# Attention scores of 96 heads on one core: blocks of eight heads for blocks of four, loads of 64 partitions for loads of 128, and all copies of a head on ScalarE

## The chip, the cores and the metric

The kernel runs on one core of one Trainium2 chip; the other cores are idle. The metric is the device time of one execution in microseconds (us): the median of ten runs before the change, and the median of the changed kernel's runs after it. One execution of each kernel is also recorded by the hardware profiler; all rows below come from that execution. Its span, from the first recorded instruction to the last, is a little shorter than its time.

## The reference

```python
batch, n_heads, seq, head_dim = 8, 12, 1024, 64
q, k: float32 [8, 12, 1024, 64]
np.einsum('bhid,bhjd->bhij', q, k).astype(np.float32)
```

For each of the 96 pairs of batch and head, 1024 query rows of 64 numbers are multiplied with 1024 key rows. The result of one head is a 1024 x 1024 matrix in float32, 4 MB. All inputs together are 50.33 MB, all outputs 402.65 MB.

## The kernel before

A "head" below is one of the 96 matrices. The kernel goes through them in order, in blocks: `sizes = [1, 1, 2, 2, ...]`, where a block with G has two halves of G heads each, so the first two blocks have 2 heads and the other 23 have 4. GMAX is 2. In a block, the heads of the first half have their transposed q and k on partitions 0 to 63 and those of the second half on 64 to 127.

The stages of a block, each on its own engine:

- **Loads** (`Block.load`, line 74). For each half and each of q and k there is one DMA into a tile `x_sb` of 128 partitions; partition p holds 8G consecutive rows of the input. For G = 2 that is 16 rows of 64 floats, 4 KB per partition, 512 KB per DMA. `in_pool` has 5 such tiles (each with q and k of one half). The first three blocks are loaded into the tile `early`, which borrows one of the output buffers.
- **Casts** (`cast_rows`, line 93, for the first two blocks, and `cast_quads`, line 115, for the others). GpSimd turns the rows into float16 in the tile `half_sb`. `cast_quads` works on 32 partitions at a time and moves each piece so that a later transpose of 32 x 32 squares gives the head's matrix transposed. `half_pool` has 2 tiles, and a block takes one.
- **Transposes** (`transpose_rows`, lines 140 and 143, for the first two blocks; `transpose_quads`, line 132, for the others). The first kind is eight TensorE transposes through PSUM and a VectorE copy. The second is a VectorE instruction, two of them for q and two for k of a block: each reads 1024 contiguous elements per partition of `half_sb` and writes them to `qT` or `kT` with a step of R = 8G elements. `tr_pool` has two tiles of each name.
- **Scores** (`scores`, line 159). For each head there are four steps u; in each, TensorE does four products of 64 x 128 by 64 x 512 into a PSUM tile of 128 x 2048 floats. There are two such tiles.
- **Copies** from PSUM to the output tile `o_sb` (128 partitions x 32 KB). ScalarE does them (line 170), except for every fourth head of a block (n = 3), which VectorE does (line 168). For the very first head the two engines share each step (lines 165 and 166). `out_pool` has four output tiles.
- **Store** (line 174). SP issues one DMA of 4 MB per head, 32 KB per partition.

The order is written out: `pin` keeps every instruction in program order on its engine, and the program itself is one loop over blocks and heads. While block i is multiplied, the transposes of block i+1 are put into its heads by the dictionary `side` (after step 0 of heads 0, 1 and 2; head 2 takes two). After the copies of a head, ScalarE issues one load (two after the first head), taken from the list `stream` of the loads of all later blocks. Six loads of this list are issued ahead of the loop, three by SP and three by ScalarE. The casts of block i+3 are put on GpSimd's queue at the end of block i. An instruction waits for its data and for its buffer to be free; the waiting instruction holds up what is queued behind it on its engine. For ScalarE a load that waits holds up the next head's copies.

Of the kernel before, what the change touches and what calls it, by code (L numbers as in the profile page):

```python
# [9 lines left out]
F16 = mybir.dt.float16  # L10
F32 = mybir.dt.float32
P = 128
# [3 lines left out]
def kernel(  # L16
# [6 lines left out]
    nc = tc.nc  # L23

    B, H, S, D = q.shape
    NT = S // P
    BH = B * H
    GMAX = 2
    assert D == 64 and NT == 8 and BH % (2 * GMAX) == 0


# [5 lines left out]
    kf = k.rearrange("b h s d -> (b h s) d")  # L37
    of = out.rearrange("b h i j -> (b h) i j")

    sizes = [1, 1] + [GMAX] * (BH // (2 * GMAX) - 1)  # L40
    assert 2 * sum(sizes) == BH
    PE_BLOCKS = 2

    consts = ctx.enter_context(tc.tile_pool(name="consts", bufs=1))
    ident = consts.tile([P, P], F16)

    in_pool = ctx.enter_context(tc.tile_pool(name="in_pool", bufs=5))
    half_pool = ctx.enter_context(tc.tile_pool(name="half_pool", bufs=2))
    tr_pool = ctx.enter_context(tc.tile_pool(name="tr_pool", bufs=2))
    out_pool = ctx.enter_context(tc.tile_pool(name="out_pool", bufs=4))  # L50
    po_pool = ctx.enter_context(
        tc.tile_pool(name="po_pool", bufs=2, space=bass.MemoryType.PSUM)
    )
# [2 lines left out]
    pin = tc.keep_in_program_order  # L56

    class Block:
# [4 lines left out]

        def load(self, n, eng):
            half, x = divmod(n, 2)
            if self.raw[half] is None:
                x_sb = in_pool.tile([P, 2, self.elems], F32, tag="x")
                self.raw[half] = x_sb  # L70
            start = (self.first + half * self.G) * S
            src = (qf, kf)[x][start : start + self.G * S]
            pin(
                eng.dma_start(  # L74
                    out=self.raw[half][:, x],
                    in_=src.rearrange("(p r) d -> p (r d)", p=P),
                )
            )

# [19 lines left out]

        def cast_quads(self, half_sb):
            self.half_sb = half_sb
            for half in range(2):
                raw = self.raw[half].rearrange(
                    "p x (r h d) -> p x r h d", h=2, d=32
                )
                for h in range(2):
                    q0 = 32 * (2 * half + h)
                    dst = half_sb[q0 : q0 + 32].rearrange(  # L110
                        "p (x b r d) -> p x b r d", x=2, b=4, d=32
                    )
                    for b in range(4):
                        pin(
                            nc.gpsimd.tensor_copy(  # L115
                                out=dst[:, :, b],
                                in_=raw[32 * b : 32 * b + 32, :, :, h],
                            )
                        )

        def alloc(self):
            self.qT = tr_pool.tile([P, GMAX * S], F16, tag="qT")
            self.kT = tr_pool.tile([P, GMAX * S], F16, tag="kT")

        def transpose_quads(self, part, x):
            src = self.half_sb.rearrange("p (x n) -> p x n", x=2)[:, x]
            src = src.rearrange("p (b r i) -> p b r i", b=4, i=32)
            dst = (self.qT, self.kT)[x].rearrange(
                "c (b i r) -> c b r i", b=4, i=32, r=self.R
            )  # L130
            two = slice(2 * part, 2 * part + 2)
            pin(nc.vector.transpose(out=dst[:, two], in_=src[:, two]))  # L132

        def transpose_rows(self, x):
            assert self.G == 1
# [7 lines left out]
            pin(nc.vector.tensor_copy(out=dst, in_=src))  # L143


        def scores(self, n, by_vector, side):
            half, g = divmod(n, self.G)
            cs = slice(half * D, (half + 1) * D)

            qT = self.qT.rearrange("c (g m t) -> c g t m", t=NT, m=P)  # L150
            kT = self.kT.rearrange("c (g j) -> c g j", j=S)
            o_sb = out_pool.tile([P, NT, S], F32, tag="out")
            for u in range(NT // 2):
                ps = po_pool.tile([P, 2, S], F32, tag="po")
                for tt in range(2):
                    for j in range(2):
                        js = slice(j * 512, (j + 1) * 512)
                        pin(
                            nc.tensor.matmul(  # L159
                                ps[:, tt, js], qT[cs, g, 2 * u + tt], kT[cs, g, js]  # L160
                            )
                        )
                dst = o_sb[:, 2 * u : 2 * u + 2]
                if self.first + n == 0:
                    pin(nc.scalar.copy(out=dst[:, 0], in_=ps[:, 0]))  # L165
                    pin(nc.vector.tensor_copy(out=dst[:, 1], in_=ps[:, 1]))  # L166
                elif by_vector:
                    pin(nc.vector.tensor_copy(out=dst, in_=ps))  # L168
                else:
                    pin(nc.scalar.copy(out=dst, in_=ps))  # L170
                if u in side:
                    side[u]()
            pin(
                nc.sync.dma_start(  # L174
                    out=of[self.first + n].rearrange("(p t) j -> p (t j)", p=P),
                    in_=o_sb.rearrange("p t j -> p (t j)"),
                )
            )

    blocks, first = [], 0  # L180
# [4 lines left out]

    early = out_pool.tile([P, NT, S], F32, tag="out")
    raw = early.rearrange("p t j -> p (t j)")  # L190
    at = 0
    for b in blocks[:3]:
        for half in range(2):
            b.raw[half] = raw[:, at : at + 2 * b.elems].rearrange(
                "p (x n) -> p x n", x=2
            )
            at += 2 * b.elems
        for n in range(4):
            b.load(n, (nc.sync, nc.scalar)[n % 2])
    stream = [(b, n) for b in blocks[3:] for n in range(4)]  # L200

    def next_load(eng):
        if stream:
            b, n = stream.pop(0)
            b.load(n, eng)

    for n in range(6):
        next_load((nc.sync, nc.scalar)[n % 2])
    make_identity(nc, ident)

    def to_half(i):
        if i < len(blocks):
            if i == 1:
                half_sb = blocks[0].half_sb[:, 4 * blocks[0].elems :]
            else:
                half_sb = half_pool.tile([P, 8 * GMAX * NT * D // 2], F16, tag="half")
            if i < PE_BLOCKS:
                blocks[i].half_sb = half_sb
                blocks[i].cast_rows(half_sb)
            else:  # L220
                blocks[i].cast_quads(half_sb)

    for i in range(3):
        to_half(i)

    blocks[0].alloc()
    for x in range(2):
# [1 line left out]
    for i, b in enumerate(blocks):  # L229
        nxt = blocks[i + 1] if i + 1 < len(blocks) else None  # L230
        if nxt:
            nxt.alloc()
        heads = 2 * b.G
        for n in range(heads):
            side = {}
            if nxt and i + 1 < PE_BLOCKS:
                side = {3: lambda: nxt.transpose_rows(n)}
            elif nxt and n < 3:
                parts = [(p, x) for p in range(2) for x in range(2)]
                some = parts[n : n + 1 + (n == 2)] if heads == 4 else parts[2 * n :][:2]  # L240
                side = {0: lambda: [nxt.transpose_quads(*s) for s in some]}
            b.scores(n, n == 3, side)
            if i == n == 0:
                next_load(nc.scalar)
            next_load(nc.scalar)
            if i == 0 and n == heads - 1:
                to_half(3)
        if i > 0:
            to_half(i + 3)


# [28 lines left out]
```

## Time and profile before

| | before |
|---|---|
| median of 10 runs | 1068.32 us (1067.97 to 1069.05) |
| the profiled execution, its own time | 1068.53 us |
| its span | 1066.8 us |
| busy TensorE (matmul) | 705.0 us, 66% |
| busy VectorE | 617.7 us, 58% |
| busy ScalarE | 528.9 us, 50% |
| busy GpSimd | 385.7 us, 36% |
| bytes moved by DMA | 453.29 MB, 425 GB/s over the span |

In the profile PE is TensorE, DVE is VectorE, ACT is ScalarE, POOL is GpSimd and SP is SyncE. A line of digits shows 40 equal slices of the span, each digit the busy share in tenths. A group's row gives the line of the kernel, the engine, the operation, output and input with partitions x elements and type, the count, then busy time and mean duration in ns, and after the second bar the engine's idle time ahead of these instructions and what ended most of it. The chain follows back from the last instruction what each step waited for. Rows of windows give, for a stretch of the span, its length, the busy time and count of TensorE's matmuls and weight loads, VectorE, ScalarE and GpSimd, TensorE's clock as a share, the busy share of the DMA engines and the GB/s that they moved.

### The profile page before, as it was taken

What the parts mean: (1) busy time and instruction counts of PE and PEld (TensorE: products, weight loads), DVE (VectorE), ACT (ScalarE), POOL (GpSimd) and SP (SyncE); (2) the same over time, 40 slices, a digit from 0 to 9 for tenths busy, and PEclk for the clock granted to TensorE, in tenths of its full rate; (3) what the DMA queues carried; (4) which work ended last, traced back from release to release, by engine and by line L of the source; (5) the groups of instructions that cost most, each with busy time, mean ns of one, the idle gap of its engine ahead of it and who ended that gap; (6) DMA issues with size and microseconds to landing.
All of it is one profiled execution on the core that took longest, in us unless ns stands there. A gap on an engine that the chain in (4) does not pass through costs nothing.

```text
span 1066.8 us, 4547 instructions
## 1 busy us (share of the span) xinstructions
PE 705.0 (66%) x1568; PEld 237.7 (22%) x1568; DVE 617.7 (58%) x192; ACT 528.9 (50%) x293; POOL 385.7 (36%) x382
## 2 busy tenths in 40 slices
PE   5997566657666675766657576675766766677750
PEld 2332122222222221222222122221222222222210
DVE  3886729366393673845738458385483754955330
ACT  3867264364543645537355373553735546447530
POOL 7894341633416334253352433524335243300000
DMA  9999999999999999999999999999999999999996
GB/s 377 428 424 436 417 423 437 427 434 430 431 429 432 431 431 431 431 428 429 431 428 432 430 431 429 432 430 426 432 429 430 430 430 431 432 434 433 431 434 276
DMA packets 28248, 453.29 MB, mean 425 GB/s; under 512 B 3136, under 2 KB 3136, under 8 KB 15936
## 3 DMA queue, kind: packets, MB, share of 16 engines
q1 hardware_dynamic: 15120, 406.33, 88.6%
q10 hardware_dynamic: 13104, 46.67, 10.8%
q8 instruction: 12, 0.20, 0.1%
q14 instruction: 12, 0.10, 0.0%
HBM read 50.33 MB, written 402.65 MB: 425 GB/s over the span
## 4 chain that ended last, share of the span: by engine, by line
DMA 76%; ACT 11%; PE 6%; DVE 3%; issue 0%; DVEq 0%; ACTq 0%; SPq 0%
DMA out_dram<-o_sb 69%; ACT o_sb L170 11%; DMA x_sb<-in_q_dram 6%; PE ps L159 5%; DVE o_sb L168 3%; DMA early<-in_k_dram 1%; DVE o_sb L166 0%; DVEq L275 0%; ACT o_sb L165 0%; ACT L165 0%; DVE kT L143 0%; PE ps L140 0%; ACTq L170 0%; SPq L174 0%; ACTq L74 0%
## 5 line engine op out<-in xcount | busy, mean ns | idle before, releaser
L159 PE MATMUL ps<-kT,qT 64*128 64x512 f16 x1536 | 701.1, 617 | 320.8 <-ACT o_sb L170 207.3
L170 ACT COPY o_sb<-ps 128x2048 f32<-128x2048 f32 x288 | 523.7, 1868 | 480.8 <-DMA out_dram<-o_sb 389.1
L115 POOL CAST half_sb<-x_sb 32x1024 f16<-32x1024 f32 x352 | 363.8, 1033 | 524.3 <-DVE kT L132 385.2
L168 DVE COPY o_sb<-ps 128x2048 f32<-128x2048 f32 x92 | 204.3, 2284 | 396.3 <-DMA out_dram<-o_sb 391.1
L159 PEld LDWEIGHTS <-qT 64*128 64x128 f16 x1536 | 234.4, 157 | 785.7 <-issue 783.4
L132 DVE STREAM_TRANSPOSE kT<-half_sb 128x1024 f16<-128x1024 f16 x46 | 218.1, 4742 | 0.0
L132 DVE STREAM_TRANSPOSE qT<-half_sb 128x1024 f16<-128x1024 f16 x46 | 212.3, 4615 | 0.0
L115 POOL CAST half_sb<-early 32x1024 f16<-32x1024 f32 x16 | 16.5, 1033 | 2.3 <-DMA early<-in_k_dram 1.6
L140 PE MATMUL ps<-ident,half_sb 128*128 128x128 f16 x32 | 3.9, 309 | 7.2 <-POOL half_sb L93 6.4
L166 DVE COPY o_sb<-ps 128x1024 f32<-128x1024 f32 x4 | 4.8, 1222 | 6.5 <-ACT o_sb L165 6.5
L165 ACT ACT_TABLE_LOAD x1 | 1.3, 1283 | 11.6 <-DMA early<-in_k_dram 11.6
L143 DVE COPY kT<-ps 128x1024 f16<-128x1024 f16 x2 | 2.4, 1220 | 7.6 <-PE ps L140 7.6
L143 DVE COPY qT<-ps 128x1024 f16<-128x1024 f16 x2 | 2.4, 1220 | 7.4 <-PE ps L140 7.4
L93 POOL CAST half_sb<-early 128x512 f16<-128x512 f32 x8 | 4.7, 613 | 3.7 <-DMA early<-in_q_dram 3.6
L165 ACT COPY o_sb<-ps 128x1024 f32<-128x1024 f32 x4 | 4.0, 1014 | 3.0 <-PE ps L159 3.0
L140 PEld LDWEIGHTS <-half_sb 128*128 128x128 f16 x32 | 3.3, 142 | 8.8 <-POOL half_sb L93 6.4
masks.py:199 POOL TENSOR_SCALAR_AFFINE_SELECT ident<-ident 128x128 f16<-128x128 f16 x1 | 0.3, 292 | 0.1
masks.py:197 POOL MEMSET ident<- 128x128 f16 x1 | 0.2, 204 | 0.3 <-POOLq L264 0.3
L264 POOL MEMSET const-float32-0.0<- 128x1 f32 x1 | 0.1, 97 | 0.2 <-issue 0.2
L264 POOL MEMSET const-bfloat16-1.0<- 128x1 bf16 x1 | 0.1, 100 | 0.0
L264 POOL MEMSET const-uint8-127<- 128x1 uint8 x1 | 0.1, 100 | 0.0
L264 POOL MEMSET const-float32-1.0<- 128x1 f32 x1 | 0.1, 98 | 0.0
## 6 DMA issues: line engine op xcount, KB each, us to landing
out_dram<-o_sb SPq DMA_DIRECT2D x96, 4096.0 KB, 36.1
x_sb<-in_k_dram ACTq DMA_DIRECT2D x44, 512.0 KB, 25.2
x_sb<-in_q_dram ACTq DMA_DIRECT2D x41, 512.0 KB, 25.6
x_sb<-in_q_dram SPq DMA_DIRECT2D x3, 512.0 KB, 10.2
early<-in_k_dram ACTq DMA_DIRECT2D x4, 256.0 KB, 5.2
early<-in_q_dram SPq DMA_DIRECT2D x4, 256.0 KB, 4.8
early<-in_q_dram SPq DMA_DIRECT2D x2, 512.0 KB, 7.2
early<-in_k_dram ACTq DMA_DIRECT2D x2, 512.0 KB, 7.3
```

Source lines behind the costliest of these rows:

```text
L93: nc.gpsimd.tensor_copy(out=self.halves[x][:, :, half], in_=self.raw[half][:, x].rearrange("p (r d) -> p r d", d=D),)
L115: nc.gpsimd.tensor_copy(out=dst[:, :, b], in_=raw[32 * b : 32 * b + 32, :, :, h],)
L132: pin(nc.vector.transpose(out=dst[:, two], in_=src[:, two]))
L140: pin(nc.tensor.transpose(t_ps[:, t], self.halves[x][:, t], ident))
L143: pin(nc.vector.tensor_copy(out=dst, in_=src))
L159: nc.tensor.matmul(ps[:, tt, js], qT[cs, g, 2 * u + tt], kT[cs, g, js])
L165: pin(nc.scalar.copy(out=dst[:, 0], in_=ps[:, 0]))
L166: pin(nc.vector.tensor_copy(out=dst[:, 1], in_=ps[:, 1]))
L168: pin(nc.vector.tensor_copy(out=dst, in_=ps))
L170: pin(nc.scalar.copy(out=dst, in_=ps))
L264: nc = _bacc.Bacc("TRN2", target_bir_lowering=False, num_devices=1)
```

## The change

- GMAX is 4: after blocks of 2, 2 and 4 heads come eleven blocks of 8 heads. A half of such a block has 8 KB per partition and input.
- A load of a half is cut into two pieces, of partitions 0 to 63 and 64 to 127, so that a DMA stays at 512 KB. There is still one load after each head, and two after heads 0, 2, 3, 4 and 5.
- `in_pool` has 3 tiles (each twice as large), `half_pool` has 3 and a block takes two of them, `out_pool` has 3.
- The casts of a half are queued as soon as its loads have been issued, up to two or three blocks ahead. They handle 32 x 2048 elements each.
- A transpose of an eight-head block handles 128 x 2048 elements and writes with a step of 32 elements. The four are put into heads 0, 2, 4 and 6 of the block before.
- ScalarE does all copies of all heads, but for the first head, which is shared as before, and one step of the second head, which VectorE does. Both transposes of the second block by TensorE are put into the second head.

```diff
-    GMAX = 2
+    GMAX = 4
...
-    sizes = [1, 1] + [GMAX] * (BH // (2 * GMAX) - 1)
+    sizes = [1, 1, 2] + [GMAX] * (BH // (2 * GMAX) - 1)
...
-    in_pool = ctx.enter_context(tc.tile_pool(name="in_pool", bufs=5))
-    half_pool = ctx.enter_context(tc.tile_pool(name="half_pool", bufs=2))
+    in_pool = ctx.enter_context(tc.tile_pool(name="in_pool", bufs=3))
+    half_pool = ctx.enter_context(tc.tile_pool(name="half_pool", bufs=3))
...
-    out_pool = ctx.enter_context(tc.tile_pool(name="out_pool", bufs=4))
+    out_pool = ctx.enter_context(tc.tile_pool(name="out_pool", bufs=3))
...
+        def pieces(self):
+            parts = 2 if self.G == GMAX else 1
+            return [(n, part, parts) for n in range(4) for part in range(parts)]
+
+        def load(self, piece, eng):
+            n, part, parts = piece
...
+            rows = slice(part * P // parts, (part + 1) * P // parts)
             pin(
                 eng.dma_start(
-                    out=self.raw[half][:, x],
-                    in_=src.rearrange("(p r) d -> p (r d)", p=P),
+                    out=self.raw[half][rows, x],
+                    in_=src.rearrange("(p r) d -> p (r d)", p=P)[rows],
                 )
             )
...
+        def cast_quads(self, half):
+            raw = self.raw[half].rearrange("p x (r h d) -> p x r h d", h=2, d=32)
+            for h in range(2):
+                q0 = 32 * (2 * half + h)
+                for b in range(4):
+                    dst = self.half_sb[b // 2][q0 : q0 + 32].rearrange(
+                        "p (x b r d) -> p x b r d", x=2, b=2, d=32
                     )
+                    pin(
+                        nc.gpsimd.tensor_copy(
+                            out=dst[:, :, b % 2],
+                            in_=raw[32 * b : 32 * b + 32, :, :, h],
                         )
+                    )
...
-                elif by_vector:
+                elif self.first + n == 1 and u == 1:
                     pin(nc.vector.tensor_copy(out=dst, in_=ps))
...
+    casts = [(i, half) for i in range(PE_BLOCKS, len(blocks)) for half in range(2)]
+
+
+    def to_half(last):
+        while casts:
+            i, half = casts[0]
+            b = blocks[i]
+            if i > last:
+                return
+            if any(sb is b and piece[0] // 2 == half for sb, piece in stream):
+                return
+            if half == 0:
+                b.half_sb = [half_tile()[:, : 2 * b.elems] for _ in range(2)]
+            b.cast_quads(half)
+            casts.pop(0)
...
-                side = {3: lambda: nxt.transpose_rows(n)}
-            elif nxt and n < 3:
+                if n == 1:
+                    side = {u: lambda x=u // 2: nxt.transpose_rows(x) for u in (1, 3)}
+            elif nxt:
                 parts = [(p, x) for p in range(2) for x in range(2)]
-                some = parts[n : n + 1 + (n == 2)] if heads == 4 else parts[2 * n :][:2]
+                some = [s for m, s in enumerate(parts) if m * heads // 4 == n]
                 side = {0: lambda: [nxt.transpose_quads(*s) for s in some]}
-            b.scores(n, n == 3, side)
-            if i == n == 0:
+            b.scores(n, side)
+            for _ in range(2 if b.first + n in (0, 2, 3, 4, 5) else 1):
                 next_load(nc.scalar)
-            next_load(nc.scalar)
-            if i == 0 and n == heads - 1:
-                to_half(3)
-        if i > 0:
-            to_half(i + 3)
+            to_half(i + 2 + (n == heads - 1))
```

More of the change, by code (lines that the diff above doesn't have):

```diff
@@ L62, in __init__ @@
             self.raw = [None] * 2
-        def load(self, n, eng):
+        def pieces(self):
[3 more added lines that the diff above has]
+            n, part, parts = piece
             half, x = divmod(n, 2)
@@ L97, in cast_rows @@
                 )
[L102 to L111, printed above, removed]
-                    )
[L113 to L118, printed above, removed]
+        def cast_quads(self, half):
[5 more added lines that the diff above has]
+                        "p (x b r d) -> p x b r d", x=2, b=2, d=32
+                    )
+                    pin(
+                        nc.gpsimd.tensor_copy(
+                            out=dst[:, :, b % 2],
+                            in_=raw[32 * b : 32 * b + 32, :, :, h],
                         )
+                    )
         def alloc(self):
@@ L125, in transpose_quads @@
         def transpose_quads(self, part, x):
-            src = self.half_sb.rearrange("p (x n) -> p x n", x=2)[:, x]
-            src = src.rearrange("p (b r i) -> p b r i", b=4, i=32)
-            dst = (self.qT, self.kT)[x].rearrange(
+            src = self.half_sb[part].rearrange(
+                "p (x b r i) -> p x b r i", x=2, b=2, i=32
+            )[:, x]
+            dst = (self.qT, self.kT)[x][:, : self.G * S].rearrange(
                 "c (b i r) -> c b r i", b=4, i=32, r=self.R
-            )
-            two = slice(2 * part, 2 * part + 2)
-            pin(nc.vector.transpose(out=dst[:, two], in_=src[:, two]))
+            )[:, 2 * part : 2 * part + 2]
+            pin(nc.vector.transpose(out=dst, in_=src))
         def transpose_rows(self, x):
@@ L143, in transpose_rows, with scores @@
             pin(nc.vector.tensor_copy(out=dst, in_=src))
-        def scores(self, n, by_vector, side):
+        def scores(self, n, side):
             half, g = divmod(n, self.G)
@@ L197 @@
             at += 2 * b.elems
-        for n in range(4):
-            b.load(n, (nc.sync, nc.scalar)[n % 2])
-    stream = [(b, n) for b in blocks[3:] for n in range(4)]
+        for n, piece in enumerate(b.pieces()):
+            b.load(piece, (nc.sync, nc.scalar)[n % 2])
+    stream = [(b, piece) for b in blocks[3:] for piece in b.pieces()]
     def next_load(eng):
         if stream:
-            b, n = stream.pop(0)
-            b.load(n, eng)
+            b, piece = stream.pop(0)
+            b.load(piece, eng)
     for n in range(6):
@@ L209, with half_tile @@
     make_identity(nc, ident)
[L211 to L224, printed above, removed]
+    def half_tile():
+        half_sb = half_pool.tile([P, 2 * GMAX * NT * D], F16, tag="half")
+        return half_sb
+    casts = [(i, half) for i in range(PE_BLOCKS, len(blocks)) for half in range(2)]
[11 more added lines that the diff above has]
+            casts.pop(0)
+    half_sb = half_tile()
+    at = 0
+    for b in blocks[:PE_BLOCKS]:
+        b.cast_rows(half_sb[:, at:])
+        at += 4 * b.elems
+    to_half(2)
     blocks[0].alloc()
```

## The prediction

> **What bounds the kernel now.** I read the page first (slices, queues, chain, groups), then the table of waits, the timeline of the first 75 us, and windows at the end. The page:
>
> ```profile
> span 1066.8 us, 4547 instructions
> ...
> DMA  9999999999999999999999999999999999999996
> GB/s 377 428 424 436 417 423 437 427 434 430 431 429 432 431 431 431 431 428 429 431 428 432 430 431 429 432 430 426 432 429 430 430 430 431 432 434 433 431 434 276
> ...
> q1 hardware_dynamic: 15120, 406.33, 88.6%
> q10 hardware_dynamic: 13104, 46.67, 10.8%
> ...
> DMA 76%; ACT 11%; PE 6%; DVE 3%; issue 0%; DVEq 0%; ACTq 0%; SPq 0%
> ...
> L170 ACT COPY o_sb<-ps 128x2048 f32<-128x2048 f32 x288 | 523.7, 1868 | 480.8 <-DMA out_dram<-o_sb 389.1
> L115 POOL CAST half_sb<-x_sb 32x1024 f16<-32x1024 f32 x352 | 363.8, 1033 | 524.3 <-DVE kT L132 385.2
> L168 DVE COPY o_sb<-ps 128x2048 f32<-128x2048 f32 x92 | 204.3, 2284 | 396.3 <-DMA out_dram<-o_sb 391.1
> ...
> L132 DVE STREAM_TRANSPOSE kT<-half_sb 128x1024 f16<-128x1024 f16 x46 | 218.1, 4742 | 0.0
> L132 DVE STREAM_TRANSPOSE qT<-half_sb 128x1024 f16<-128x1024 f16 x46 | 212.3, 4615 | 0.0
> ```
>
> The DMA engines are over 90% busy in 39 of 40 slices, and the two big queues (q1: stores and a few loads, q10: loads) fill 99.4% of sixteen engines' span. Both copying engines wait mostly for a store to free an output buffer. So the kernel is bound by the bytes and by what the DMA engines pay per packet; all compute is cover. The end shows the rest:
>
> ```profile
> 1040.00:1050.00 10.00, 0.00 (x0) 0.00 (x0) 0.00 (x0) 0.00 (x0) 0.00 (x0) 1.00 1.00 429
> 1050.00:1055.00 5.00, 0.00 (x0) 0.00 (x0) 0.00 (x0) 0.00 (x0) 0.00 (x0) 1.00 0.93 400
> 1055.00:1060.00 5.00, 0.00 (x0) 0.00 (x0) 0.00 (x0) 0.00 (x0) 0.00 (x0) 1.00 0.38 164
> 1060.00:1066.80 6.80, 0.00 (x0) 0.00 (x0) 0.00 (x0) 0.00 (x0) 0.00 (x0) 1.00 0.09 40
> ```
>
> The last two columns are the DMA share and GB/s: computing is over by 1036, and the sixteen engines finish apart. By the trace's landings, the last store ends on the first engine at 1054.8 and on the last at 1065.0. **The slowest DMA engine sets the end**, and it never idles.
>
> The trace's packet records give prices: 4 KB load packets 159 ns (most; mean 161), 32 KB store packets 1213 ns (mean 1217), 2 KB packets 84 ns, and a dozen 8 KB instruction fetches 309 ns at their most frequent. That is 75 ns per 2 KB and 9 ns per packet.
>
> [...]
>
> **The change, part by part.**
>
> *Copies.* 91 of VectorE's 92 copies of 2048 elements go to ScalarE: 91 x 1.868 = 170 us, ACT 529 to 699 us busy, DVE loses about 208. In the timeline ScalarE makes a head in 7.65 us (38.81 to 46.46); a head's DMA takes 4.19 MB store plus 0.52 MB load at 430 GB/s = 10.97 us. So production keeps 3.3 us per head, and the cost is nothing while DMA hides it. Cover gone, a kernel at ScalarE's pace would need 96 x 7.65 = 734 us.
>
> *Three output buffers for four.* A buffer is free when its store has landed; the copies end some 7.6 us later, while two other stores drain (2 x 10.97 = 21.9 us). Fast engines lead the slowest by up to 10.2 us, which leaves about 4 us with loads and, at 9.75 us a head, 1.7 us in the tail. If it fails, only fast engines idle. Cost nothing.
>
> *Loads.* 100 loads as before. 88 of them go from 128 packets of 4 KB to 64 of 8 KB: 88 x 64 = 5632 fewer packets, x 9 ns / 16 engines = **3.2 us less** on every engine. They stay on ScalarE's queue behind each head's copies, with two per head after heads 0, 2, 3, 4 and 5. Each waits for the casts that free its buffer; behind it on ScalarE stand the next head's copies, and behind those TensorE's two score buffers and SP's store. The worst such wait that I find: the second load after head 3 needs casts of the first half of block 3. GpSimd starts these at 29.9, does two, waits for kT's first transposes of block 2 (done at 40.0), and does six more of 2.1 us (2 x 1.075, from 16 in 17.2 us): 52.6. Head 3's copies end at 46.4, so ScalarE stands 6 us; the stores of heads 2 and 3 keep DMA busy until about 68. Cost nothing.
>
> *Port sharing.* Four packets per engine and load, so 88 x 4 = 352 packets of 8 KB per engine; [...] The trace doesn't show this, so the bounds are zero (sharing can't speed anything up) and full lockstep, 352 x 309 ns = **109 us**. Between them: a load packet alternates with a store packet, cycle 309 + 1213 = 1522 ns. With offsets spread evenly two engines overlap with chance 618/1522 = 0.41 and lose 155 ns on average: 63 ns per packet, 22 us in all. Before 200 us the engines are more in step: in the records of 100 to 200 us, 12.8 of 15 other engines start a load packet within 309 ns of a given one, in 300 to 500 us 7.4 of 15, which is near even. For some 18 loads I take 200 ns a packet (14 us), for 70 loads 63 ns (18 us): 32 us. The slowest pair decides and the mean doesn't; against that stands its slack of some microseconds. I take **35 us**.
>
> *Casts and transposes.* Casts of 2048 elements, half as many: the same 365 us. 44 transposes of 2048 and 4 of 1024 in place of 92 of 1024. The step of the writes goes from 32 to 64 bytes[...]. I take 4.6 ns per element: 9.36 us each, 37.4 of the 88 us that 8 heads take. Bounds: not below the price per element seen, and up to twice it, 18.7 us each and 75 of 88 us. At the start the first eight-head block has least room: casts of its first tile end at 40 + 12 x 2.1 = 65.2, the four transposes at 102.6. Head 10, the first that needs the last two, is due when stores through head 9 drain: 41.9 + 15.2 MB at 428 GB/s, about 135 us. Nothing at 9.36 us.
>
> *Start and tail.* Both transposes of block 1 fall in head 1, and VectorE takes one of head 1's copies. Loads queued at once (7.3 MB, 17 us) reach to 19.6 and store 0 starts at 21; store 1 is issued near 30.5 before store 0 has drained. I put it at nothing, with 2 us either way. The last head is copied by ScalarE in 7.5 us, under the drain of two stores: nothing.
>
> Sum: span 1066.8 - 3.2 + 35 = 1098.6. The profiled execution took 1068.53, 1.7 outside its span, and the median is 0.2 under it: 1100.1, **1100 us**.
>
> **The rivals.** *A, my forecast:* port sharing, 1100; by itself 1075 to 1140. [...] against it: the alternation with long stores, which can hold two writers apart. *B, not slower:* the ports don't bind[...], and only the dearer packets go: 1068.3 - 3.2 = 1065.1. It decides if port sharing costs under 1 us: loads are 11% of the bytes. *C:* they cancel, with port sharing of about 3 us: 1068. *D:* transposes at 64-byte steps are dear. Head 10 is late once 65.2 + 4t + 9.5 passes 135, t over 15 us; at 18.7 it is ready at 149.5, 14 us late once, and with port sharing absent 1068.3 - 3.2 + 14 = 1079. [...] That the change doesn't do what it says: the instruction order shows packets of 64 x 2048 elements, so it does.
>
> **How the numbers follow.** A 0.60, B 0.29, C 0.05, D 0.06. About 0.2% (2 us) is what a measurement of this kernel can tell from no change. Faster: B but for 0.02, 0.27. Same: C and that rest, 0.07. Slower: A and D, 0.66. Range: from B with 2 us for the start, 1063, to 1135, which leaves out about 0.05 below and 0.12 above, where the lockstep end of A lies.
>
> **What would show it.** Packets of 8 KB at 309 ns and a load queue near 10.5% of the span: B. Longer load packets, a load queue well over 11%, GB/s under 425 in the middle slices and back to 432 after the last load: A. Transposes at 9.4 us and no TensorE wait for kT around 80 to 140 us: D is wrong. DMA digits under 9 in the middle would mean production starves it, by a wait I missed. I am wrong if middle slices hold 431 or more.

## The result, and the profile after

| | before | changed |
|---|---|---|
| median | 1068.35 us | 1078.48 us (8 runs, 1077.59 to 1080.85) |
| ratio, with its 95% interval | 1 | 1.0098 [1.0089, 1.0107] |
| span of the profiled execution | 1066.8 us | 1076.3 us |
| packets of stores, per DMA engine, summed | 934.9 us | 941.4 us |
| packets of loads, per DMA engine, summed | 124.1 us | 126.9 us |

The change makes the kernel slower by 10 us, where 32 were forecast: the right sign, and a third of the size. The last two rows are sums over the trace's packet records, divided by sixteen engines. They rise by 9.3 us together, and the span by 9.5: **the whole loss lies in packets that take longer**, not in engines that stand idle. From the page of the changed kernel:

```profile
span 1076.3 us, 4312 instructions
...
DMA  9999999999999999999999999999999999999996
GB/s 289 420 430 430 427 434 431 428 432 426 430 421 431 423 424 431 421 429 427 420 432 425 425 429 424 428 433 427 421 433 428 425 424 434 431 432 432 433 429 295
...
q1 hardware_dynamic: 14928, 406.33, 88.6%
q10 hardware_dynamic: 7664, 46.67, 10.8%
...
L173 ACT COPY o_sb<-ps 128x2048 f32<-128x2048 f32 x379 | 689.2, 1869 | 343.7 <-DMA out_dram<-o_sb 312.1
L118 POOL CAST half_sb<-x_sb 32x2048 f16<-32x2048 f32 x176 | 332.5, 1889 | 527.3 <-DMA x_sb<-in_k_dram 490.9
...
L135 DVE STREAM_TRANSPOSE qT<-half_sb 128x2048 f16<-128x2048 f16 (+1 forms) x24 | 214.1, 8919 | 481.4 <-issue 461.4
L135 DVE STREAM_TRANSPOSE kT<-half_sb 128x2048 f16<-128x2048 f16 (+1 forms) x24 | 216.8, 9034 | 0.0
```

The DMA digits are as full as before, yet the first slice moves 289 GB/s for 377, and the middle slices lie between 420 and 434. The busy share doesn't show the loss: in the first windows below it is 1.04 at 421 GB/s and 1.03 at 294; the GB/s do. The load queue has nearly half its packets (7664 for 13104) and the same share of time. ScalarE still waits mainly for stores (312.1 of its 343.7 us idle), so it doesn't bind. Three windows each, the kernel before and then the changed one (the last two columns are the DMA share and GB/s):

```profile
10.00:30.00 20.00, 16.19 (x48) 6.46 (x46) 6.10 (x6) 12.00 (x9) 16.67 (x17) 1.00 1.04 421
450.00:600.00 150.00, 100.02 (x220) 33.32 (x218) 79.70 (x25) 76.05 (x42) 59.44 (x58) 1.00 1.01 430
880.00:960.00 80.00, 56.89 (x125) 18.91 (x124) 49.43 (x16) 41.48 (x24) 16.53 (x16) 1.00 1.00 432
```

```profile
10.00:30.00 20.00, 13.19 (x37) 5.03 (x36) 8.32 (x6) 7.10 (x6) 16.58 (x16) 1.00 1.03 294
450.00:600.00 150.00, 99.46 (x221) 33.76 (x220) 72.71 (x8) 98.32 (x55) 47.13 (x25) 1.00 1.00 426
880.00:960.00 80.00, 58.28 (x129) 19.81 (x128) 36.35 (x4) 59.44 (x33) 8.62 (x5) 1.00 1.00 432
```

So there are **two losses**. At the start, while there is hardly a store yet, the rate falls by 127 GB/s for 20 us: 2.5 MB, 6 us. In the middle it is 1% lower; after the last load nothing is lost. The packet records say which packets: before 30 us the 8 KB load packets take 529 ns on average, where 309 is their price; from 200 to 880 us load packets are nearly at their price (311 ns), and the 32 KB store packets between them rise from 1217 to 1230 ns.

### The profile page after: what moved, and what is told of

The parts are those of the page before. It is cut to its first block, busy times and chain, and to the rows that moved or that the text cites. A ratio compares the mean times of both kernels' runs of the same rounds, so it can differ in the third digit from the quotient of the medians.

```text
span 1076.3 us, 4312 instructions
## 1 busy us (share of the span) xinstructions
PE 700.7 (65%) x1568; PEld 240.5 (22%) x1568; DVE 429.2 (40%) x57; ACT 694.5 (65%) x384; POOL 354.6 (33%) x206
## 3 DMA queue, kind: packets, MB, share of 16 engines
q10 hardware_dynamic: 7664, 46.67, 10.8%
## 4 chain that ended last, share of the span: by engine, by line
DMA 73%; ACT 17%; PE 7%; DVE 1%; issue 0%; ACTq 0%
DMA out_dram<-o_sb 72%; ACT o_sb L173 17%; PE ps L162 6%; DMA early<-in_k_dram 1%; DVE o_sb L169 0%; DVE o_sb L171 0%; PE ps L143 0%; ACT o_sb L168 0%; ACT L168 0%; DVE kT L146 0%; DVE qT L146 0%; ACTq L173 0%; ACTq L81 0%
## 5 line engine op out<-in xcount | busy, mean ns | idle before, releaser
L173 ACT COPY o_sb<-ps 128x2048 f32<-128x2048 f32 x379 | 689.2, 1869 | 343.7 <-DMA out_dram<-o_sb 312.1
L118 POOL CAST half_sb<-x_sb 32x2048 f16<-32x2048 f32 x176 | 332.5, 1889 | 527.3 <-DMA x_sb<-in_k_dram 490.9
L162 PEld LDWEIGHTS <-qT 64*128 64x128 f16 x1536 | 237.2, 157 | 799.6 <-issue 797.0
L135 DVE STREAM_TRANSPOSE qT<-half_sb 128x2048 f16<-128x2048 f16 (+1 forms) x24 | 214.1, 8919 | 481.4 <-issue 461.4
L135 DVE STREAM_TRANSPOSE kT<-half_sb 128x2048 f16<-128x2048 f16 (+1 forms) x24 | 216.8, 9034 | 0.0
L169 DVE COPY o_sb<-ps 128x1024 f32<-128x1024 f32 x4 | 4.8, 1222 | 7.1 <-ACT o_sb L168 7.1
L171 DVE COPY o_sb<-ps 128x2048 f32<-128x2048 f32 x1 | 2.3, 2292 | 2.0 <-PE ps L162 2.0
```

The costliest lines, as they stand in the source:

```text
L118: nc.gpsimd.tensor_copy(out=dst[:, :, b % 2], in_=raw[32 * b : 32 * b + 32, :, :, h],)
L135: pin(nc.vector.transpose(out=dst, in_=src))
L162: nc.tensor.matmul(ps[:, tt, js], qT[cs, g, 2 * u + tt], kT[cs, g, js])
```

## The experiments

My theory after the result: loads into partitions 0 to 63 or 64 to 127 alone make the DMA engines hold each other up, at the start and in the middle. "Port sharing" and "ports", in the prediction and in the expectations, are my names for this assumption; no row above shows what the engines wait for. Rivals: buffers or ScalarE's order starve the DMA engines; packets of 8 KB as such lengthen the stores; any cut of the loads into more DMAs costs. The kernels ran on different chips; the kernel before, which ran beside each of them, is at 1068.1 to 1068.7 us on each, so their times can be compared to about 1 us.

### Whole loads, cut loads, buffers

**e1_whole**, the changed kernel with whole loads:

```diff
             n, part, parts = piece
+            if part == 1:
+                return
+            parts = 1
```

> The changed kernel, but each input's half is loaded by one DMA of 128 partitions x 8 KB (1 MB) where its first piece stood, and nothing is issued at the second piece's place. Theory[...]: the two losses vanish, first 8 KB loads from about 525 ns per packet back to about 309, store packets in the middle from 1230 ns back to 1217, and what is left is the saving of 9 ns x 352 packets: 1068.3 - 3.2 = 1065 us. Rival 1 (three output buffers, ScalarE copies or the new order starve the DMA engines): no change, 1076 to 1079. Rival 2 (packets of 8 KB themselves make the store packets between them longer): the start is repaired, the middle is not, about 1072.

Measured: **1064.89 us**, ratio 0.9967 [0.9954, 0.9979]. The windows:

```profile
10.00:30.00 20.00, 15.80 (x48) 6.09 (x46) 8.64 (x7) 9.11 (x7) 16.74 (x17) 1.00 1.04 434
450.00:600.00 150.00, 100.29 (x222) 34.35 (x222) 67.62 (x8) 100.94 (x56) 52.82 (x28) 1.00 1.00 431
880.00:960.00 80.00, 59.67 (x133) 20.20 (x131) 36.30 (x4) 59.94 (x34) 0.00 (x0) 1.00 1.00 433
```

Both losses are gone (434 and 431 GB/s; store packets 1218 ns), and the saving in packets is there. The kernel beats both others. Buffers, copies, casts and transposes are those of the changed kernel, so Rivals 1 and 2 fall.

**e4_before_3buf_act** asks the same from the other side: the kernel before with `bufs=3` for `out_pool` and `b.scores(n, False, side)`.

> The kernel before, with three output buffers for four and all copies of every head but the first by ScalarE; loads, casts and transposes as before. Theory: both are hidden under the stores, 1068 to 1069 us. Rival 1 (they starve the DMA engines): 1072 to 1078.

Measured: 1069.11 us, ratio 1.0009 [1.0001, 1.0016]: 0.7 us, and 0.1 to 1.7 by the interval.

**e2_before_cut**, the kernel before with its loads cut:

```diff
+            cut = 2 if self.first >= 8 else 1
+            for part in range(cut):
+                rows = slice(part * P // cut, (part + 1) * P // cut)
...
-                    out=self.raw[half][:, x],
-                    in_=src.rearrange("(p r) d -> p (r d)", p=P),
+                    out=self.raw[half][rows, x],
+                    in_=src.rearrange("(p r) d -> p (r d)", p=P)[rows],
```

> The kernel before, with each load from the fourth block on cut into two DMAs of 64 partitions x 4 KB (256 KB each); buffers, copies, casts and transposes as before. Port sharing alone, with no packet saved: about 5 us lost at the start (six loads with 8 packets per engine, each some 100 ns longer) and 6 us in the middle, 1068.3 + 11 + 1 for the added completion writes = 1080 us. If port sharing isn't the cause: 1068 to 1070.

Measured: 1085.57 us, ratio 1.0155 [1.0142, 1.0168], 17 us over before and more than expected. Here the load packets themselves carry it (140.4 us per engine for 124.1, stores 935.7 for 934.9): at the start 195 to 280 GB/s, in the middle 174 ns for 159. The cut alone is enough to make the loss. (The 1 us that was expected on top stands for small packets: in the trace of before each DMA has sixteen of 4 bytes, of 9 ns each.)

**e3_first_whole** and **e7_first_cut** split it in time: only the first eight-head block's loads whole, and only they cut. Each is the edit of e1_whole under `if self.first == 8:` and `if self.first > 8:`.

> The changed kernel, with whole loads for the first eight-head block alone (the loads that run while there is no store yet); all later loads stay cut. Theory: the start's share returns, 5 to 6 us: 1078.5 - 5.5 = 1073 us, store packets in the middle stay at 1230 ns. Rival (the start's loss is made up later anyhow, or comes from the new order of head 1): 1078.

> The complement of the kernel with the first eight-head block whole: only that block's loads are cut, all later ones are whole. If the two losses add up: 1064.9 + 4 (what making the first block whole brought) to + 6 (by the packets) = 1069 to 1071 us, store packets in the middle near 1218 ns. If an early lag stays and costs more later: above 1072.

Measured: 1074.43 us (1.0046 [1.0034, 1.0058]) and 1071.61 us (1.0030 [1.0018, 1.0041]). The windows of e7_first_cut:

```profile
10.00:30.00 20.00, 13.60 (x38) 5.13 (x36) 8.32 (x6) 7.29 (x7) 16.54 (x16) 1.00 1.03 289
450.00:600.00 150.00, 98.83 (x218) 33.41 (x216) 72.69 (x8) 97.93 (x55) 45.36 (x25) 1.00 1.00 430
```

The start's loss is there alone, the middle at 430. From both sides the start's share is 4 to 7 us (1078.5 - 1074.4, 1071.6 - 1064.9), and the middle's 7 to 10.

### Which partitions: DMAs by themselves

**m1_rates** and **m2_parts** are DMAs alone, in stretches with a fence between them. A stretch of m2_parts is

```python
for low, high in ((0, 64), (32, 96), (64, 128), (0, 32), (0, 96), (0, 128)):
    fence()
    for n in range(16):
        load(n, low, high)
```

> A kernel of loads alone (it computes nothing and stores one head of zeros): stretches of 16 loads each, one queue, 8 KB per partition, into partitions 0-63, 32-95, 64-127, 0-31, 0-95 and 0-127; then 128 partitions of 4 KB; then 0-63 again with source rows 16 KB apart. Theory[...]: 206 to 218 GB/s for 0-63 and 64-127 and with the spread source rows, about 200 for 0-31, and about 420 for 32-95[...]. Rival 1 (any DMA of 64 partitions is slow, because of how its rows are dealt to the engines): 32-95 is as slow as 0-63. Rival 2 (the rows' places in HBM): 0-63 with spread source rows is fast, or 128 partitions of 4 KB are slow.

The windows of m2_parts, one for each stretch in the order of the expectation (VectorE and GpSimd, then clock, DMA share, GB/s):

```profile
20.00:60.00 40.00, 0.00 (x0) 0.00 (x0) 1.00 1.01 204
82.00:101.00 19.00, 0.00 (x0) 0.00 (x0) 1.00 0.97 398
121.00:162.00 41.00, 0.00 (x0) 0.00 (x0) 1.00 0.99 201
182.00:201.00 19.00, 0.00 (x0) 0.00 (x0) 1.00 1.02 204
221.00:273.00 52.00, 0.00 (x0) 0.00 (x0) 1.00 1.00 240
294.00:333.00 39.00, 0.00 (x0) 0.00 (x0) 1.00 1.00 419
353.00:373.00 20.00, 0.00 (x0) 0.00 (x0) 1.00 1.00 395
394.00:433.00 39.00, 0.00 (x0) 0.00 (x0) 1.00 1.00 205
```

Partitions 0-63, 64-127 and 0-31 run at 201 to 204 GB/s with the DMA share at 1; **32-95, as many partitions, at 398**, with packets of 317 ns on average for 641. Spread source rows change nothing (205). Both rivals fall: which partitions a load fills decides its rate, and 64 partitions from 0 on are no faster than 32 (204 GB/s both). What the engines wait for while a packet takes 641 ns is not shown. For 0-95, which ran at 240 GB/s, I had no expectation.

> A kernel of DMAs alone (it computes nothing; it stores zeros for 32 of the 96 heads): 32 loads of partitions 0 to 63, 8 KB each; then 32 loads alternating 0-63 and 64-127 on one queue; then 16 whole loads of 128 x 8 KB; then 16 stores of 4 MB on SP beside 32 cut loads on ScalarE's queue; then 16 stores beside 16 whole loads. [...] cut loads 618 ns per packet and 218 GB/s alone in both orders; [...] about 525 ns and 254 GB/s, as at the start of the changed kernel. Whole loads 309 ns and 430 GB/s. Beside stores, if offsets between engines stay as they begin (in step), each load packet costs some 200 ns more to the end of the stretch, 14% of the rate; if the stores move the engines apart, the loss falls to about 30 ns per packet after the first few, as in the middle of the changed kernel.

From m1_rates: the two stretches of cut loads alone, whole loads, and the stretch of stores with cut loads from its beginning on (its first window has the fence in it):

```profile
20.00:100.00 80.00, 6.46 (x1) 0.00 (x0) 1.00 1.02 207
120.00:190.00 70.00, 6.88 (x1) 0.00 (x0) 1.00 1.01 220
220.00:250.00 30.00, 3.65 (x1) 0.00 (x0) 1.00 1.01 424
270.00:290.00 20.00, 11.64 (x2) 0.00 (x0) 1.00 0.76 179
290.00:300.00 10.00, 0.00 (x0) 0.00 (x0) 1.00 0.94 395
300.00:310.00 10.00, 0.00 (x0) 0.00 (x0) 1.00 1.01 418
310.00:330.00 20.00, 0.00 (x0) 0.00 (x0) 1.00 1.00 428
```

Cut loads alone: 639 ns per packet, and 601 when halves alternate: 207 and 220 GB/s, 6% more. Half rate (twice 309 ns, 618) is right, and 525 ns is not. But beside stores the load packets fall from 606 ns (280 to 290 us, almost no store) to 310, 339 and 311 in the next three windows of 10 us, and what the store packets take over 1213 ns falls from 48 ns to 0 by 320 us. **The loss does not last once long stores stand between the loads.** Later in the stretch, from 370 to 380 us, there is hardly a store again, and the loads take 570 ns.

### Partitions in the middle of the kernel, and a second cause

**e5_middle** and **e6_lower** cut at other places:

```diff
-            rows = slice(part * P // parts, (part + 1) * P // parts)
+            cuts = ([(32, 96)], [(0, 32), (96, 128)])[part]   # e5_middle
+            cuts = ([(0, 64)], [(64, 96), (96, 128)])[part]   # e6_lower
```

> The changed kernel with the cuts laid elsewhere: the first piece is partitions 32 to 95[...], the second piece is two DMAs, 0 to 31 and 96 to 127[...]. Theory (ports): [...] about half of the 13.6 us between the changed kernel and the one with whole loads goes: 1078.5 - 6.8 = 1072 us. Rival (the cut into smaller DMAs is what costs, whatever the partitions): 1078 to 1080, the same as the next kernel.

> The control for the kernel before it: as many DMAs of the same sizes, but the pieces are 0 to 63, and then 64 to 95 and 96 to 127[...]. Theory (ports): 1078 to 1080 us, six to seven over the other cut. Rival (the number and size of DMAs costs): the two are equal.

Measured: 1082.87 us (1.0135 [1.0120, 1.0151]) and 1083.84 us (1.0147 [1.0131, 1.0162]): equal within their intervals, a miss. The pair was a poor test: e5_middle's second piece is two DMAs of 32 partitions, of which 0-31 ran at 204 GB/s in m2_parts, and at the start it runs beside the first piece on the other queue. Still, in the middle the store packets of e5_middle are no shorter than those of e6_lower (1232 and 1231 ns), a first sign that the slow partitions alone don't make them long. Both kernels are also 4 to 5 us over the changed kernel, which has two DMAs per load for their three; where that comes from was not followed up.

**e9_same_middle** and **e10_same_lower** are the clean test: the start is whole, and both pieces go into the same 64 partitions, 32-95 (398 GB/s by themselves in m2_parts) or 0-63 (204).

```diff
-            rows = slice(part * P // parts, (part + 1) * P // parts)
+            rows = slice(32, 32 + 64) if parts == 2 else slice(0, P)   # e9; 0 for 32 in e10
```

> The changed kernel with the first three half loads whole; from then on both pieces of a load go into partitions 32 to 95[...], the second over the first a head later, and the casts read these partitions twice. It leaves out the other half of these rows; bytes, packets, DMAs and instructions are those of the changed kernel. Theory (ports): as with whole loads, 1065 to 1066 us, store packets in the middle near 1217 ns. Rival (a DMA of 64 partitions beside stores costs, whatever the ports): 1074, as its control.

> The control: the same with both pieces into partitions 0 to 63[...]; it leaves out the other half of these rows too. Theory (ports): 1073 to 1075 us, some 9 us over the other, store packets in the middle near 1230 ns. Rival: the two are equal.

Measured: 1070.12 us (1.0020 [1.0010, 1.0029]) and 1075.06 us (1.0065 [1.0051, 1.0078]), on one chip. The middle windows, e9_same_middle first:

```profile
450.00:600.00 150.00, 97.75 (x216) 33.45 (x216) 67.99 (x8) 99.61 (x55) 45.31 (x24) 1.00 1.00 428
```

```profile
450.00:600.00 150.00, 97.24 (x215) 33.12 (x214) 71.78 (x8) 95.47 (x53) 45.31 (x24) 1.00 1.00 424
```

Which 64 partitions the loads fill makes 5 us of difference. In the packet records it lies mostly in the load packets, 321 ns for 310 between 200 and 880 us; the store packets are at 1231 and 1228. So with loads into 32-95 e9_same_middle has nearly the long store packets of the changed kernel (1230), and it is still 5 us above whole loads, which my theory did not have.

**e8_columns** cuts along the row instead (`cols` of the row for `rows`, 128 partitions x 4 KB).

> The changed kernel with each load cut along the row instead of along the partitions: two DMAs of 128 partitions x 4 KB, 512 KB as before, one after each head. Theory (ports): no sharing, and the saving in packets is gone too: 1064.9 + 3.2 = 1068 us, loads at 159 ns and stores in the middle at about 1217 ns. Rival (any cut of the loads, or this many DMAs, lengthens the stores): 1074 or more.

Measured: 1069.86 us, ratio 1.0021 [1.0005, 1.0037]; stores 1216 ns, loads 159.6 ns. More DMAs as such don't lengthen the stores; the saving in packets is gone. Its middle window:

```profile
450.00:600.00 150.00, 98.00 (x216) 33.50 (x216) 68.00 (x8) 99.88 (x55) 45.34 (x24) 1.00 1.01 431
```

**e11_spread**, **e12_whole_again** and **e13_middle_again** ran on one chip: e9_same_middle with spread source rows (`"(p t r) d -> t p (r d)"`, every other row), whole loads, and e9_same_middle.

> As the kernel with both pieces into partitions 32 to 95, but each piece takes every other 8 KB row of the half's 1 MB in HBM, 16 KB apart, instead of 64 rows in one run (it leaves out the right pairing of rows and partitions, and half of the partitions). If the place of the rows in HBM lengthens the stores between them: 1065 to 1067 us, store packets in the middle near 1218 ns. If not: 1070, as without the spreading, near 1228 ns.

> Whole loads again, for comparison on one chip: 1065 us. If the chips differ by the 5 us in question: 1068 to 1070.

> Both pieces into partitions 32 to 95 again, on the same chip as whole loads (it leaves out the other half of these rows): 1070 us if loads of 64 partitions lengthen the stores without sharing a port, 1065 to 1066 if it was the chip.

Measured: 1069.88 us (1.0017 [1.0007, 1.0028]), 1065.37 us (0.9981 [0.9970, 0.9992]) and 1069.96 us (1.0015 [1.0008, 1.0021]). The 4.6 us are real on one chip, and the rows' place in HBM is not their cause.

**e14_pairs** and **e15_after_pairs** change the rhythm: two pieces after every second head. In e14_pairs q's and k's piece are also put next to each other in the list.

```diff
-            for _ in range(2 if b.first + n in (0, 2, 3, 4, 5) else 1):
+            head = b.first + n
+            loads = 2 if head in (0, 2, 3, 4, 5) else 1
+            if head > 8:
+                loads = 2 * (head % 2)
+            for _ in range(loads):
```

> As the kernel with both pieces into partitions 32 to 95, but q's and k's piece are issued together after every second head instead of one after each, which is the rhythm of the whole loads (it leaves out the other half of the rows, as that kernel does). If the rhythm lengthens the stores: 1065 to 1066 us and store packets near 1218 ns in the middle. If the shape of the DMA does: 1070, 1228 ns.

> The changed kernel, its loads as they are, but from the ninth head on both pieces of a load are issued together after every second head. If the rhythm counts: the start's loss of 6 us stays and most of the middle's goes, 1072 to 1074 us. If it doesn't: 1078 to 1079.

Measured: 1065.75 us (0.9975 [0.9965, 0.9986]), store packets 1222 ns, and 1075.10 us (1.0058 [1.0045, 1.0072]). The middle windows of e13_middle_again and e14_pairs:

```profile
450.00:600.00 150.00, 96.60 (x215) 33.02 (x214) 68.98 (x8) 98.41 (x55) 45.26 (x24) 1.00 1.00 427
```

```profile
450.00:600.00 150.00, 99.51 (x220) 34.11 (x220) 66.64 (x8) 99.90 (x56) 49.80 (x27) 1.00 1.01 429
```

With the whole loads' rhythm, loads into 32-95 cost nearly as little as whole ones (1065.75 us for 1065.37): **the second loss goes with the rhythm**. The rhythm alone is not enough for it: the kernel before and e8_columns issue one DMA of 512 KB after each head too, of 128 partitions x 4 KB, and their store packets stay at 1217 and 1216 ns. So it takes the shape of these loads as well, 64 partitions x 8 KB; which of the two, the partitions or the packet size, was not tried. And e14_pairs changes the order of the pieces as well; the order was not tried by itself.

In e15_after_pairs, where only the rhythm changes, it brings 3 us, but its store packets stay at 1229 ns. Of the 2.2 us by which its span is shorter than that of the changed kernel, the packets of loads and stores account for 0.4; where the rest comes from is not shown. Against whole loads, with the start's 6 us taken off where it is cut:

| middle of the kernel | one piece after each head | two after every second |
|---|---|---|
| loads into 32-95 | +5 (e9, e13) | +1 (e14) |
| loads into 0-63 and 64-127, or 0-63 | +7 to +10 (the changed kernel: 1078.5 - 6 - 1065; e3, e10) | about +4 (e15: 1075.1 - 6 - 1065) |

So the slow partitions cost some 2 to 5 us in the middle and the rhythm 3 to 6; the runs don't part them more closely. How the rhythm lengthens the store packets (1228 ns in e9_same_middle for 1222 in e14_pairs) is not shown.

## Why the prediction was wrong

**What bounds the kernel, and the saving**: right. The packets fill all but some 2 to 8 us of the span in each kernel that computes the scores. The saving in packets was put at 3.2 us; e1_whole is 3.5 us under the kernel before and e12_whole_again 3.1.

**Copies, buffers, loads on ScalarE's queue, transposes**: right. Copies and three buffers together cost 0.7 us (e4_before_3buf_act). The wait that I worked out behind head 3 is in the timeline: the second load after it is issued at 54.97 and the next head's copies begin at 55.62, after casts; the DMA share there is 1. Transposes of 2048 elements took 9.31 us for qT and 9.42 for kT, against 9.36; at either step that is 4.5 to 4.6 ns an element, so a step of 64 bytes costs no more than one of 32 here, and rival D is out. Casts took 1.89 us against 2.1.

**Port sharing**: in the prediction an assumption that no row of before showed. The runs show that loads into 0-63 or 64-127 go at half rate by themselves (204 and 201 GB/s; 641 ns a packet for the 317 of 32-95), and not what the engines wait for. The size is where the prediction failed. The step is "For some 18 loads I take 200 ns a packet (14 us), for 70 loads 63 ns (18 us): 32 us."

- *The first term.* The 200 ns a packet were right (529 - 309 = 220), the 18 loads were not. The records lose 6.2 us per engine before 30 us, in some 7 loads, when there is hardly a store, and 0.4 us in load packets from 30 to 100 us, where I still charged 200 ns. I took the closeness of starts in the kernel before for a lockstep that lasts, and with it the loss. m1_rates shows that the loss doesn't last: loads that alternate with stores fall from 606 to about 310 ns within some 10 us.
- *The second term.* 18 us were charged for the middle. Measured: store packets 1230 for 1217 ns, 13 ns x 8 packets x 62 heads between 200 and 880 us = 6.4 us, and 0.6 us in load packets over 309 ns. Most of this is not what the term stands for: with loads into 32-95 the store packets are already at 1227 to 1228 ns (e9, e13). By the table, the slow partitions cost 2 to 5 us in the middle; the rest comes with the rhythm, which the prediction didn't have.
- *The 3 us for the slowest pair* did not come: the spans grow by the mean of the packet sums (9.3 and 9.5).

In its place: 6 us at the start + 7 to 10 in the middle (partitions and rhythm) - 3.2 saved = 10 to 13 us, where 10 were measured. That the change is slower was forecast for a reason that holds, slow loads into half of the partitions at the start (529 ns a packet for 309); their cost in the middle came in part from something else.

The sign that I named, a load queue well over 11%, did not show: it stayed at 10.8%, as in the middle the store packets carry the loss. The GB/s in the middle fell, but to 426 in the window and not under 425. That they come back to 432 after the last load did show.

## What to carry to other kernels

A DMA into half of the partitions ran at half rate here or did not, and which half decided: 0-63 was slow (204 GB/s), 32-95 was not (398). Larger packets were to be had with whole loads of 128 partitions instead (1064.89 us). Read GB/s beside the DMA share, which was 1.01 at 204 GB/s and 0.97 at 398. Charge such a loss where the transfers run by themselves (639 ns a packet in m1_rates), above all before the first store, and don't multiply its worst price by every transfer between long stores (310 ns).

## What the runs showed of the hardware that was not expected

- Longer store packets were no mark of the slow partitions here: they are 1228 ns in e9_same_middle, whose loads go into 32-95, and 1230 in the changed kernel. What the slow partitions add shows mostly in the load packets: 321 ns for 310 in e10_same_lower, and with 4 KB loads 174 for 159 in e2_before_cut (stores 1220).
- 96 partitions from 0 on are little better than 64: 240 GB/s for 204 in m2_parts.
- The same bytes in the same packets cost 4 us more as one DMA of 64 partitions after each head than as two after every second (1069.96 and 1065.75 us); with DMAs of 128 partitions x 4 KB, one after each head doesn't lengthen the stores (1216 ns in e8_columns).
